# Accumulating three of the seven block products of a down projection in PSUM, in another order

## Chip, cores and metric

The kernel runs on one core of one Trainium2 chip. The metric is the device time of one execution in microseconds (us), the median of several runs.

## The reference

One layer of a causal decoder trunk on 1072 positions (16 meta tokens, 1024 prompt tokens, 8 x 4 new tokens), model width 1024, hidden width 2816:

```python
def swiglu(x, wg, wu, wd):
    return (jax.nn.silu(x @ wg) * (x @ wu)) @ wd
...
x = x + 0.5 * swiglu(rmsnorm(x, g1), w1g, w1u, w1d)
h = rmsnorm(x, gm)
...
x = x + jnp.concatenate([c, q], axis=-1) @ w_out + b_out
x = x + 0.5 * swiglu(rmsnorm(x, g2), w2g, w2u, w2d)
```

The change lies in the last product of the two SwiGLUs, the one with `wd`, the "down" product, and in its addition to x with the factor 0.5. All values are fp32.

## The kernel before

**Layout.** x is held transposed: channels on the 128 partitions (8 tiles of channels), positions along the free axis in three pieces of 358. `X(k, piece)` is one 128x358 tile of x. Each fp32 matrix operand is split into a high and a low part (`split`, L142 to L144: ScalarE casts the high part, VectorE or GpSimd subtracts it from the source for the low part), and a product is three matmuls per tile: high x high, high x low, low x high (`mul`, L129). For weights the low part is always made by GpSimd (`half_unit`, L167).

**Passes.** The first SwiGLU runs on the first two pieces of x in one pass, then on the third piece; the second one on its first piece and then on the other two in one pass. The passes on two pieces (`fast_pass`, L1095; "fast") save multiplications: a product of 2x2 blocks is made from seven block products m1 to m7 in place of eight, with sums of weight blocks and of data blocks as operands. `block_steps` (L522) takes the four weight blocks a11, a12, a21, a22 of such a product (two DMAs of 256 KB at a time), makes the sums on VectorE (`sums`, L534: L540 makes s1, L541 the operand of m7, L542 that of m6, L543 that of m3; m5 takes s1, m4 takes a22, m1 and m2 the raw a11 and a12) and hands each block product on.

**The down products.** In a fast pass, four pairs of hidden tiles after one another form a group with the following pair (`GROUPS`, L71), so there are four groups in each of the two passes. A group's hidden values are the data blocks b11, b21, b22, and the sums t1 to t4, made by `group_sink` (L679) as the up product of the group's second pair comes out. The names of the data operands in the profile are `xb` (b11 and b21), `hid0` and `hid1` (t2), `hid2` and `dt3l` (t3: high part in hid2, low part in dt3l), `dt1` (t1), `dt4` (t4), `db22` (b22). t3 is the last chain: VectorE subtracts b11's high part (L691) and its low part (L692) from b22's, ScalarE casts `hid2`, VectorE makes `dt3l` (L144). For each of two tiles i there is one such chain; that of i = 0 is made last and is the first one a product reads.

`fast_down` (L606) makes the down products of a group, once for each half j of the output channels: two blocks for each group, 16 in all. A block has seven products of two output tiles (`mp`) each, and each of these has six matmuls and takes one PSUM bank; there are eight banks (`pp`, L89). `OPERAND_OF` (L560) says which data operand a product takes. When a product is done, VectorE adds it to x at one or two places (L618), which the table `ADDS` (L603) lists. (A "twist" of x on GpSimd before and after the groups, L622, makes these additions enough.)

**Order.** `put_blocks` (L1079) puts the products in the order m1 with m2, m6, m7, m5, m4, m3 (`USUAL`, L1077). In `fast_pass` the gate product of the pair after the group stands ahead of the group's down products, and that pair's up product behind them. The planner loop (L1291) makes the weight operands of a step two steps ahead of its matmuls; there are six buffers for split weights (`W_BUFS`) and eight for raw blocks (`R_BUFS`). TensorE runs its matmuls in the order written (`keep_in_program_order`); the framework puts the instructions of the other engines in an order of its own by when it takes them to be ready, and each engine then works strictly in that order.

The gate product of the next pair leaves its results in PSUM: VectorE adds them up (L570) and ScalarE takes the Silu from the bank (L696, or L668 for a pair outside a group), which frees it.

Of the kernel before, what the change touches and what calls it, by code (L numbers as in the profile page):

```python
# [12 lines left out]
ALU = mybir.AluOpType  # L13
# [4 lines left out]
KH = KD // 2  # L18
# [66 lines left out]
def trunk(ctx: ExitStack, tc: tile.TileContext, xt, wf1, win, wout, wf2, wpool, vec, eye, sconv, spool,  # L85
          yt, ncp, npp, ncs, nps):
    nc = tc.nc
# [20 lines left out]
    def X(k, piece):  # L108

        a, b = piece  # L110
        return x[a // N][:, k, a % N : a % N + b - a]
# [8 lines left out]
    def accum():  # L120
        return pp.tile([P, 512], F32, name="acc", tag="acc")

    state = {"hid": -1, "raw": 0, "made": 0, "clock": 0.0}

    def matmul(acc, lhs, rhs, start, stop):
        tc.keep_in_program_order(nc.tensor.matmul(acc, lhs, rhs, start=start, stop=stop))  # L126
        state["clock"] += acc.shape[-1] / 2400.0

    def mul(accs, parts, start=True, stop=True):  # L129


        last = len(parts) - 1
        for i, (wh, wl, rh, rl) in enumerate(parts):
            for j, (lhs, rhs) in enumerate(((wh, rh), (wh, rl), (wl, rh))):
                at = 0
                for c, acc in enumerate(accs):
                    n = acc.shape[-1]
                    moving = rhs[c] if isinstance(rhs, list) else rhs[:, at : at + n]
                    matmul(acc, lhs, moving, start and i == 0 and j == 0, stop and i == last and j == 2)
                    at += n  # L140

    def split(hi, lo, src, engine=None):  # L142
# [376 lines left out]
            ups.append([plain(wsrc[4 * (f // 2) + f % 2], gate), plain(wsrc[4 * (f // 2) + 2 + f % 2], up)])  # L519
        return ups, [down_steps(wsrc, p, [piece], hid) for p in range(PAIRS)]  # L520

    def block_steps(src0, src1, product):  # L522

        st = {}

        def make0():
            st["r0"] = take(), take()
            return tuple(half_unit(r) for r in st["r0"])

        def use0(w):  # L530
            product("m1", w[0])
            product("m2", w[1])

        def sums():  # L534

            if "m4" in st:
                return
            (a11, a12), a21, a22 = st.pop("r0"), take(), take()
            s1 = pools["fast"].tile([P, KH, P], F32, name="sx", tag="sx", bufs=2)
            nc.vector.tensor_tensor(s1, a21, a22, ALU.add)  # L540
            nc.vector.tensor_tensor(a21, a11, a21, ALU.subtract)  # L541
            nc.vector.tensor_tensor(a11, s1, a11, ALU.subtract)  # L542
            nc.vector.tensor_tensor(a12, a12, a11, ALU.subtract)  # L543
            st.update(m5=s1, m6=a11, m7=a21, m3=a12, m4=a22)

        def made(name):
            def make():
                sums()
                return half_unit(st[name])
            return make  # L550

        def use_of(name):
            return lambda w: product(name, w)

        out = {"m12": ("step", [[(0, src0)]], make0, use0, False), "raw": [(0, src1)]}
        for name in ("m6", "m7", "m5", "m4", "m3"):
            out[name] = ("step", [], made(name), use_of(name), True)
        return out
# [3 lines left out]
    def fast_pair(src0, src1, get, n, sink):  # L562
# [23 lines left out]
        def product(name, w):  # L586
# [13 lines left out]

    ADDS = {"m1": ((0, 0, 1), (1, 1, 1)), "m2": ((0, 0, 1),), "m6": ((1, 1, 1),), "m7": ((1, 1, 1), (0, 1, 1)),  # L603
            "m5": ((1, 1, 1), (1, 0, 1)), "m4": ((1, 0, -1),), "m3": ((0, 1, -1),)}

    def fast_down(wsrc, p, j, pieces, ops):  # L606

        unit0 = 2 * F_TILES + 2 * p + 2 * j
        n = pieces[0][1] - pieces[0][0]

        def product(name, w):
            rh, rl = ops[OPERAND_OF[name]]
            for mp in range(2):
                acc = accum()[:, :n]
                mul([acc], [(w[0][:, 2 * mp + k], w[1][:, 2 * mp + k], rh[k], rl[k]) for k in range(2)])
                for r, c, sign in ADDS[name]:
                    to = X(j * KH + 2 * mp + r, pieces[c])
                    nc.vector.scalar_tensor_tensor(to, acc, 0.5 * sign, to, ALU.mult, ALU.add)  # L618

        return block_steps(wsrc[unit0], wsrc[unit0 + 1], product)  # L620

    def twist(pieces):  # L622

# [6 lines left out]
    def fast_ffn(wsrc, pieces, free, get, hid):  # L630
# [3 lines left out]
        n = N  # L634
# [44 lines left out]
        def group_sink(ops, second):  # L679
            silus, hs = {}, {}  # L680
            sub = nc.vector.tensor_tensor

            def put(name, i, t):
                if not ops:
                    ops.update(borrowed())
                if name not in ops:
                    ops[name] = own(name, 0), own(name, 1)
                split(ops[name][0][i], ops[name][1][i], t)

            def less(t, s, name, i):  # L690
                sub(t, s, ops[name][0][i], ALU.subtract)  # L691
                sub(t, t, ops[name][1][i], ALU.subtract)  # L692

            def gate(i, c, t):
                silus[i, c] = kept()
                nc.scalar.activation(silus[i, c], t, AF.Silu)  # L696

            def up(i, c, t):
                h = hs[i, c] = t if c else silus[i, c]
                nc.vector.tensor_tensor(h, t, silus[i, c], ALU.mult)  # L700
                if second:
                    put("b22" if c else "b21", i, h)
                elif c == 0:
                    put("b11", i, h)
                if (i, 1 - c) not in hs:
                    return
                if not second:
                    sub(hs[i, 1], hs[i, 1], hs[i, 0], ALU.subtract)
                    put("t1", i, hs[i, 1])
                    return  # L710
                b21, b22, t3 = hs[i, 0], hs[i, 1], temp()[:, :n]
                less(b22, b22, "t1", i)
                put("t2", i, b22)
                less(t3, b22, "b11", i)
                put("t3", i, t3)
                sub(b21, b21, b22, ALU.subtract)
                put("t4", i, b21)

            return gate, up

        for p in range(PAIRS):
            start = p if p in GROUPS else p - 1
# [288 lines left out]
    def got(key, what="h"):  # L1011
        def get():
            while what not in box[key] or (what != "pool" and not tasks[key].done):
                run_background(1, False)
            return box[key][what]
        return get
# [57 lines left out]
    fb1, fb1_d = plain_ffn(wf1, FFN1_B, got("h1b"))  # L1074
    fa2, fa2_d = plain_ffn(wf2, FFN2_A, got("h2a"))
    fb2, fb2_d, _ = fast_ffn(wf2, FFN2_B, 0, got("s2", "ops"), hid_b2)
    USUAL = ("m12", "m6", "m7", "m5", "m4", "m3")  # L1077

    def put_blocks(blocks, names=USUAL):  # L1079
        for name in names:  # L1080
            step = blocks[name]
            if blocks["raw"] is not None and name != "m12":
                step = (step[0], [blocks["raw"]]) + step[2:]
                blocks["raw"] = None
            plan.append(step)

    def put_down(d):

        for half in d:
            if isinstance(half, dict):  # L1090
                put_blocks(half)
            else:
                plan.append(half)

# [105 lines left out]
    last, room = {}, {}  # L1200
# [88 lines left out]
    i = 0  # L1289
# [103 lines left out]
```

## Time and profile before

| | |
|---|---|
| median of 3 runs | 1804.93 us (1803.71 to 1805.0) |
| profiled execution, its own time | 1803.07 us |
| its span, first to last instruction | 1801.3 us |
| mean granted TensorE clock | 0.986 |
| busy: TensorE, VectorE, ScalarE, GpSimd | 96%, 77%, 42%, 64% of the span |
| additions of down products to x (L618) | 320, busy 145.0 us |

The busy shares are means over the whole span. TensorE's share counts a stretch as busy while any matmul is in flight. A matmul of 358 columns shows some 328 ns in flight, and the next one starts about 164 ns after it, so the starts of matmuls tell more than their durations. An engine's idle time is shown with what ended it.

### The profile page before, as it was taken

The page shows a single profiled execution, that of the slowest core. Times are in us where ns is not written, and L with a number is a line of the kernel's source. Part 1 is how long each engine was busy: PE and PEld are TensorE (multiplying, and loading weights), DVE is VectorE, ACT ScalarE, POOL GpSimd, SP SyncE. Part 2 cuts the span into 40 slices and gives each one's busy share as a digit, 9 for nine tenths or more (in the row PEclk, how much of TensorE's full clock was granted, in tenths as well). Part 3 has the DMA queues.
Part 4 walks back from the last instruction along what each step waited for, and adds up shares of the span by engine and source line. Part 5 has one row for each costly group of instructions (what it writes and reads, how often), then busy time and mean ns, then how long its engine had stood idle before and what let it go on. Part 6 is the DMA issues. An engine that isn't in the chain of part 4 may idle for free.

```text
span 1801.3 us, 29876 instructions
## 1 busy us (share of the span) xinstructions
PE 1729.7 (96%) x10486; PEld 1712.5 (95%) x10486; DVE 1378.4 (77%) x2621; ACT 760.3 (42%) x1482; POOL 1146.0 (64%) x894
## 2 busy tenths in 40 slices
PE   6799999999999999999999998999999999999997
PEld 6799999999999999999999998999999999999997
DVE  8869898989747795897235888538587989898965
ACT  6444444443435224434234433545353434444444
POOL 5576766667745337667346657666577676767683
PEclk9899999999999999999999999999999999999998
DMA  6122232223353223443234494444332222222232
GB/s 209 35 83 71 71 103 82 72 77 98 103 118 119 65 67 115 124 135 111 66 106 129 126 135 133 126 134 123 111 105 91 71 83 71 82 71 72 70 100 83
DMA packets 115893, 177.70 MB, mean 99 GB/s; under 512 B 28320, under 2 KB 35744, under 8 KB 115744
## 3 DMA queue, kind: packets, MB, share of 16 engines
q1 hardware_dynamic: 115744, 175.80, 33.4%
q8 instruction: 83, 1.36, 0.3%
q14 instruction: 66, 0.54, 0.1%
HBM read 170.60 MB, written 5.15 MB: 98 GB/s over the span
## 4 chain that ended last, share of the span: by engine, by line
PE 75%; DVE 17%; issue 4%; DMA 2%; POOL 1%; ACT 1%; SPq 0%; DVEq 0%; POOLq 0%; ACTq 0%
PE acc L126 75%; DMA wraw<-in_wf 2%; DVE acc L265 2%; POOL wl L144 1%; DVE acc L814 1%; DVE wraw L542 1%; DVE acc L570 1%; DVE wraw L541 1%; DVE tmp L570 1%; DVE tmp L692 1%; DVE x L489 1%; DVE tmp L265 1%; DVE pr L832 1%; DVE wraw L543 0%; DVE xb L144 0%
## 5 line engine op out<-in xcount | busy, mean ns | idle before, releaser
L144 POOL TENSOR_TENSOR wl<-wraw,wh 128x512 fp32r<-128x512 f32 x740 | 991.3, 1350 | 588.9 <-ACT wh L143 541.7
L143 ACT CAST wh<-wraw 128x512 fp32r<-128x512 f32 x740 | 453.6, 621 | 685.6 <-PE acc L126 455.5
L126 PE MATMUL acc<-smt,wh 128*128 128x358 f32 x1024 | 253.1, 328 | 5.0 <-DVE mixl L144 4.0
L126 PEld LDWEIGHTS acc<-smt,wh 128*128 128x128 f32 x1024 | 181.7, 190 | 6.3 <-DVE mixl L144 4.6
L814 DVE SCALAR_TENSOR_TENSOR acc<-ub,vecs,acc 128x340 f32<-128x340 f32 (+2 forms) x348 | 183.5, 571 | 2.6
L126 PE MATMUL acc<-mixlt,wh 128*128 128x340 f32 x704 | 165.6, 319 | 2.6 <-DVE smt L144 2.4
L126 PE MATMUL acc<-smt,wl 128*128 128x358 f32 x512 | 167.8, 328 | 0.0
L489 DVE SCALAR_TENSOR_TENSOR x<-acc,x 128x358 f32<-128x358 f32 (+1 forms) x240 | 119.4, 517 | 35.0 <-PE acc L126 34.2
L618 DVE SCALAR_TENSOR_TENSOR x<-acc,x 128x358 f32<-128x358 f32 x320 | 145.0, 516 | 0.5 <-PE acc L126 0.4
L570 DVE TENSOR_TENSOR acc<-tmp,acc 128x358 f32<-128x358 f32 x168 | 85.7, 527 | 51.5 <-PE acc L126 48.2
L126 PEld LDWEIGHTS acc<-mixlt,wh 128*128 128x128 f32 x704 | 120.9, 188 | 3.4 <-DVE smt L144 2.7
L126 PE MATMUL acc<-mixlt,wl 128*128 128x340 f32 x352 | 112.1, 319 | 0.8 <-POOL wl L144 0.8
L144 POOL TENSOR_TENSOR wl<-sx,wh 128x512 fp32r<-128x512 f32 x58 | 85.5, 1475 | 30.5 <-ACT wh L143 28.7
L126 PEld LDWEIGHTS acc<-smt,wl 128*128 128x128 f32 x512 | 96.9, 189 | 0.0
L542 DVE TENSOR_TENSOR wraw<-sx,wraw 128x512 f32<-128x512 f32 x58 | 78.1, 1347 | 11.8 <-POOL wl L144 11.6
L126 PE MATMUL acc<-mixh,wh 128*128 128x356 f32 (+1 forms) x320 | 79.3, 328 | 4.7 <-DVE mixl L144 2.7
L126 PE MATMUL acc<-mixl,wh 128*128 128x356 f32 (+1 forms) x320 | 78.6, 327 | 0.0
L126 PE MATMUL acc<-mixh,wl 128*128 128x356 f32 (+1 forms) x320 | 78.5, 327 | 0.0
L541 DVE TENSOR_TENSOR wraw<-wraw 128x512 f32<-128x512 f32 x58 | 77.0, 1327 | 0.4
L570 DVE TENSOR_TENSOR tmp<-tmp,acc 128x358 f32<-128x358 f32 x126 | 65.4, 519 | 14.3 <-PE acc L126 13.1
L126 PE MATMUL acc<-b11h,wh 128*128 128x358 f32 x184 | 61.7, 335 | 10.8 <-ACT wh L143 10.8
L543 DVE TENSOR_TENSOR wraw<-wraw 128x512 f32<-128x512 f32 x58 | 70.4, 1214 | 2.0 <-POOL wl L144 1.5
(286 smaller groups left out, 4762.1 us busy)
## 6 DMA issues: line engine op xcount, KB each, us to landing
wraw<-in_wf SPq DMA_DIRECT2D x544, 256.0 KB, 2.9
wraw<-in_win SPq DMA_DIRECT2D x48, 256.0 KB, 2.7
wraw<-in_wout SPq DMA_DIRECT2D x32, 256.0 KB, 2.9
x<-in_xt SPq DMA_DIRECT2D x8, 179.0 KB, 4.3
tmp<-in_xt SPq DMA_DIRECT2D x8, 179.0 KB, 2.8
x<-in_xt SPq DMA_DIRECT2D x1, 1432.0 KB, 7.0
x<-in_xt SPq DMA_DIRECT2D x8, 178.0 KB, 5.0
out_yt<-tmp SPq DMA_DIRECT2D x8, 170.0 KB, 3.3
```

The costliest lines, as they stand in the source:

```text
L126: tc.keep_in_program_order(nc.tensor.matmul(acc, lhs, rhs, start=start, stop=stop))
L143: nc.scalar.copy(hi, src)
L144: (engine or nc.vector).tensor_tensor(lo, src, hi, ALU.subtract)
L265: nc.vector.scalar_tensor_tensor(t, X(k, piece), col(gain, k), r, ALU.mult, ALU.mult)
L489: nc.vector.scalar_tensor_tensor(X(m, piece), acc, 0.5, X(m, piece), ALU.mult, ALU.add)
L541: nc.vector.tensor_tensor(a21, a11, a21, ALU.subtract)
L542: nc.vector.tensor_tensor(a11, s1, a11, ALU.subtract)
L543: nc.vector.tensor_tensor(a12, a12, a11, ALU.subtract)
L570: nc.vector.tensor_tensor(t, s, acc, ALU.add)
L618: nc.vector.scalar_tensor_tensor(to, acc, 0.5 * sign, to, ALU.mult, ALU.add)
L692: sub(t, t, ops[name][1][i], ALU.subtract)
L814: nc.vector.scalar_tensor_tensor(to, src, w, part, ALU.mult, ALU.add)
```

## The change

In the down products (not in the gate and up products) m2 is accumulated in the PSUM bank that already holds m1, m3 in the bank of m7, and m4 in the bank of m5. VectorE adds m1, m7 and m5 to one place of x while they stand alone, and once more, to another place, when the second product has been accumulated on them. The order becomes m1, m7, m5, m2, m6, m3, m4. Two subtractions have their operands exchanged, so that m3 and m4 are added and not subtracted. m1 and m2 become steps of their own, though their weights are still split together.

```diff
-    def matmul(acc, lhs, rhs, start, stop):
-        tc.keep_in_program_order(nc.tensor.matmul(acc, lhs, rhs, start=start, stop=stop))
+    def matmul(acc, lhs, rhs, start, stop, more=False):
+        tc.keep_in_program_order(nc.tensor.matmul(acc, lhs, rhs, start=start, stop=stop, skip_group_check=more))
...
-    def block_steps(src0, src1, product):
+    def block_steps(src0, src1, product, turned=False):
...
-            nc.vector.tensor_tensor(a12, a12, a11, ALU.subtract)
+            nc.vector.tensor_tensor(a12, *((a11, a12) if turned else (a12, a11)), ALU.subtract)
...
-        out = {"m12": ("step", [[(0, src0)]], make0, use0, False), "raw": [(0, src1)]}
+        def make1():
+            st["w"] = make0()
+            return st["w"][0]
+
+        out = {"m12": ("step", [[(0, src0)]], make0, use0, False), "raw": [(0, src1)],
+               "m1": ("step", [[(0, src0)]], make1, use_of("m1"), False),
+               "m2": ("step", [], lambda: st["w"][1], use_of("m2"), False)}
...
-    ADDS = {"m1": ((0, 0, 1), (1, 1, 1)), "m2": ((0, 0, 1),), "m6": ((1, 1, 1),), "m7": ((1, 1, 1), (0, 1, 1)),
-            "m5": ((1, 1, 1), (1, 0, 1)), "m4": ((1, 0, -1),), "m3": ((0, 1, -1),)}
+
+    ADDS = {"m1": (1, 1), "m2": (0, 0), "m6": (1, 1), "m7": (1, 1), "m5": (1, 1), "m4": (1, 0), "m3": (0, 1)}
+    ON = {"m2": "m1", "m3": "m7", "m4": "m5"}
...
+        banks = {}
 
         def product(name, w):
             rh, rl = ops[OPERAND_OF[name]]
+            on = ON.get(name)
             for mp in range(2):
-                acc = accum()[:, :n]
-                mul([acc], [(w[0][:, 2 * mp + k], w[1][:, 2 * mp + k], rh[k], rl[k]) for k in range(2)])
-                for r, c, sign in ADDS[name]:
-                    to = X(j * KH + 2 * mp + r, pieces[c])
-                    nc.vector.scalar_tensor_tensor(to, acc, 0.5 * sign, to, ALU.mult, ALU.add)
-
-        return block_steps(wsrc[unit0], wsrc[unit0 + 1], product)
+                acc = banks[name, mp] = banks[on, mp] if on else accum()[:, :n]
+                mul([acc], [(w[0][:, 2 * mp + k], w[1][:, 2 * mp + k], rh[k], rl[k]) for k in range(2)],
+                    on is None, True, more=on is not None)
+                r, c = ADDS[name]
+                to = X(j * KH + 2 * mp + r, pieces[c])
+                nc.vector.scalar_tensor_tensor(to, acc, 0.5, to, ALU.mult, ALU.add)
+
+        return block_steps(wsrc[unit0], wsrc[unit0 + 1], product, True)
...
-                sub(b21, b21, b22, ALU.subtract)
+                sub(b21, b22, b21, ALU.subtract)
...
+    DOWN = ("m1", "m7", "m5", "m2", "m6", "m3", "m4")
     USUAL = ("m12", "m6", "m7", "m5", "m4", "m3")
...
-            if blocks["raw"] is not None and name != "m12":
+            if blocks["raw"] is not None and name not in ("m12", "m1"):
...
-                put_blocks(half)
+                put_blocks(half, DOWN)
```

## Rows read from the trace of the kernel before

**Rows 1.** The page's first part: busy time of each engine and its share.
```profile
PE 1729.7 (96%) x10486; PEld 1712.5 (95%) x10486; DVE 1378.4 (77%) x2621; ACT 760.3 (42%) x1482; POOL 1146.0 (64%) x894
```
**Rows 2.** Windows over the eight first blocks (j = 0): start:end, length, busy (count), clock.
```profile
240.26:256.94 16.68, 14.83 (x86) 13.68 (x85) 15.87 (x29) 9.01 (x19) 12.14 (x10) 1.00 0.32 96
...
1510.75:1526.30 15.55, 14.32 (x86) 13.74 (x85) 14.95 (x25) 6.51 (x13) 10.91 (x8) 1.00 0.22 69
...
1680.90:1698.35 17.45, 15.95 (x86) 15.26 (x85) 17.24 (x29) 6.99 (x14) 12.43 (x9) 0.90 0.20 62
sum 126.71, PE 116.54 PEld 111.46 DVE 123.46 ACT 54.46 POOL 89.11; mean PE 14.57 PEld 13.93 DVE 15.43 ACT 6.81 POOL 11.14
```
**Rows 3.** The same over the eight second blocks (j = 1).
```profile
1698.35:1712.14 13.79, 13.79 (x86) 13.79 (x85) 13.24 (x26) 4.15 (x7) 11.34 (x11) 1.00 0.24 76
sum 113.92, PE 112.67 PEld 110.80 DVE 112.64 ACT 34.32 POOL 93.06; mean PE 14.08 PEld 13.85 DVE 14.08 ACT 4.29 POOL 11.63
```
**Rows 4.** Timeline of TensorE in one group: start, length, operation, count, idle before.
```profile
1510.77 0.50 PE L126 MATMUL acc<-xb,wh 128*128 128x358 f32 x2
...
1517.35 0.43 PE L126 MATMUL acc<-hid0h,wh 128*128 128x358 f32 x1 [1.23 <-ACT cc L696]
...
1518.44 0.33 PE L126 MATMUL acc<-hid2h,wh 128*128 128x358 f32 x1
1518.60 0.32 PE L126 MATMUL acc<-dt3l,wh 128*128 128x358 f32 x1
...
1528.65 0.56 PE L126 MATMUL acc<-xb,wh 128*128 128x358 f32 x2 [0.20 <-DVE x L618]
```
**Rows 5.** Timeline of VectorE in that group.
```profile
1487.39 0.54 DVE L570 TENSOR_TENSOR acc<-tmp,acc 128x358 f32<-128x358 f32 x1 [3.48 <-PE acc L126]
...
1510.60 0.68 DVE L541 TENSOR_TENSOR wraw<-wraw 128x512 f32<-128x512 f32 x1
1511.20 1.62 DVE L692 TENSOR_TENSOR tmp<-tmp,xb 128x358 f32<-128x358 f32 x1
...
1513.18 1.19 DVE L144 TENSOR_TENSOR dt4l<-cc,dt4h 128x358 fp32r<-128x358 f32 x1
...
1514.73 1.18 DVE L144 TENSOR_TENSOR dt3l<-tmp,hid2h 128x358 fp32r<-128x358 f32 x1
...
1517.58 3.58 DVE L618 SCALAR_TENSOR_TENSOR x<-acc,x 128x358 f32<-128x358 f32 x8
```
**Rows 6.** Timeline of VectorE, t3's low part in the second group of pass one.
```profile
240.81 0.53 DVE L144 TENSOR_TENSOR dt3l<-tmp,hid2h 128x358 fp32r<-128x358 f32 x1
```
**Rows 7.** Instructions of single lines: count, shortest/median/longest in ns, first and last start.
```profile
L618 DVE SCALAR_TENSOR_TENSOR x<-acc,x x320: 512/515/532, 162.2 to 1714.8; 128x358 f32<-128x358 f32 x160
...
L692 DVE TENSOR_TENSOR tmp<-tmp,xb x16: 519/1312/1623, 148.0 to 1681.7; 128x358 f32<-128x358 f32 x16
...
L144 DVE TENSOR_TENSOR dt3l<-tmp,hid2h x8: 534/1176/1181, 159.4 to 1685.2; 128x358 fp32r<-128x358 f32 x8
```
**Rows 8.** Timeline of GpSimd beside those VectorE instructions.
```profile
1510.76 1.67 POOL L144 TENSOR_TENSOR wl<-wraw,wh 128x512 fp32r<-128x512 f32 x1 [0.95 <-PE acc L126]
```
**Rows 9.** Windows of 12 us that begin with a long wait of TensorE.
```profile
553.20:565.20 12.00, 9.80 (x60) 9.50 (x59) 8.49 (x17) 8.10 (x20) 7.38 (x6) 1.00 0.27 91
584.60:596.60 12.00, 9.33 (x47) 8.80 (x46) 6.94 (x14) 3.63 (x9) 4.12 (x3) 0.86 0.15 49
821.80:833.80 12.00, 10.24 (x54) 9.83 (x52) 9.58 (x19) 4.37 (x9) 9.27 (x9) 0.86 0.38 110
856.80:868.80 12.00, 9.94 (x62) 9.44 (x61) 4.95 (x10) 4.96 (x10) 3.57 (x3) 1.00 0.16 55
994.00:1006.00 12.00, 9.60 (x60) 9.33 (x59) 7.58 (x15) 6.53 (x14) 7.54 (x6) 1.00 0.32 96
1241.60:1253.60 12.00, 9.33 (x51) 9.05 (x50) 12.00 (x26) 6.79 (x15) 7.01 (x7) 0.86 0.35 109
```

More of the change, by code (lines that the diff above doesn't have):

```diff
@@ L123, in trunk, with mul @@
     state = {"hid": -1, "raw": 0, "made": 0, "clock": 0.0}
-    def matmul(acc, lhs, rhs, start, stop):
-        tc.keep_in_program_order(nc.tensor.matmul(acc, lhs, rhs, start=start, stop=stop))
+    def matmul(acc, lhs, rhs, start, stop, more=False):
+        tc.keep_in_program_order(nc.tensor.matmul(acc, lhs, rhs, start=start, stop=stop, skip_group_check=more))
         state["clock"] += acc.shape[-1] / 2400.0
-    def mul(accs, parts, start=True, stop=True):
+    def mul(accs, parts, start=True, stop=True, more=False):
         last = len(parts) - 1
@@ L138, in mul @@
                     moving = rhs[c] if isinstance(rhs, list) else rhs[:, at : at + n]
-                    matmul(acc, lhs, moving, start and i == 0 and j == 0, stop and i == last and j == 2)
+                    matmul(acc, lhs, moving, start and i == 0 and j == 0, stop and i == last and j == 2,
+                           more)
                     at += n
```

## The prediction

> **What bounds the kernel now.** The page's first part comes first: TensorE is busy 96% of the span, VectorE 77% [rows 1]. Work taken off VectorE is worth only what TensorE now waits for it, so the next view is the length of each stretch that the change touches. Each of the 16 down blocks has 84 matmuls. The one block without a wait lasts 13.79 us, 0.164 us for a matmul [rows 3]. The eight first blocks of the groups (j = 0) last 126.71 us together [rows 2], 16.4 more than 8 x 13.79; the eight second ones 113.92 [rows 3], 3.6 more. So 20.0 us of waits stand in all down blocks, 1.1% of the span, and that is the most that relief of VectorE can give.
>
> The timelines of one group tell what these waits are. The first block begins at 1510.77. At 1517.35 TensorE has idled 1.23 us for the Silu of the gate product before it [rows 4]: the sixth PSUM bank that the block asks for still holds a gate result. VectorE is behind by then, with work of the up and gate products; it begins the first addition to x at 1517.58 [rows 5]. So none of this group's additions stands ahead of that wait, and those of the group before don't either, since VectorE idled 3.48 us until 1487.39 [rows 5]. Only the wait in the second block, at 1528.65, is one for additions to x (0.20 us of idle, released by L618) [rows 4].
>
> **Additions.** Ten additions become seven, times two output tiles and 16 blocks: 320 less 224 leaves 96 fewer. Eight of them in a row take 3.58 us [rows 5], each lasts 0.515 [rows 7], so one follows another after (3.58 - 0.52) / 7 = 0.44 us, and VectorE is relieved of 42 us. What comes of that on TensorE's path is the wait of the second blocks: 3.6 us before, of which I leave 0.5 for small matmuls of the next pass's norm that run inside one of them (an estimate). Term: **-3.1 us**. The rest of the 42 us is idle time of an engine that TensorE doesn't wait for. The first blocks' waits don't move by it.
>
> **Order.** m7 moves from fourth to second place, and its data operand is t3. In the group shown m7 reads t3 at 1518.44 and 1518.60 (high and low part) [rows 4], long after VectorE has made the low part, which it begins at 1514.73 and ends 1.18 later, at 1515.91 [rows 5]. In second place m7's first matmul would be due 12 x 0.164 after 1510.77, at 1512.74, and the second, which reads that low part, at 1512.90. It can't start before 1515.97 (0.06 for the signal, an estimate). All of TensorE's queue stands behind that matmul: m7, m5, m2, m6, m3, m4 and the up product. The delay is 3.07 us; with two slow restarts of about 0.1 each, 3.3. The bank at 1517.35 is no second wait then, since the sixth bank would be asked for at 1510.77 + 30 x 0.164 + 3.3 = 1519.0. So 3.3 us takes the place of the 1.76 us (15.55 - 13.79) that a regular first block loses now [rows 2].
>
> Of the eight low parts of t3, seven look like this one: the median lasts 1176 ns [rows 7], and the last begins at 1685.2 [rows 7], 4.3 us after its block's start at 1680.90 [rows 2]. In the second group of pass one it begins at 240.81 and lasts 0.53 [rows 6], 0.55 after the block's start [rows 2]; there is no new wait, and the block keeps the 2.9 us of bank waits that it has (16.68 - 13.79) [rows 2]. New first blocks: 7 x 3.3 + 2.9 = 26.0 against 16.4. Term: **+9.6 us**.
>
> **The clock.** A long wait of TensorE is in some cases followed by a stretch at the lower of its two levels (1.2 in place of 2.4 GHz). Of the six windows that begin with a wait of about 2 to 3 us, three have a mean granted clock of 0.86 and three of 1.00 [rows 9]. One of the eight first blocks has such a stretch now: 17.45 us long, granted 0.90 [rows 2], which is 1.7 us of clock lost at most; I take 1.5. Seven new waits at one chance in two: **+5.2 us**, with 0 and 10.5 as ends. (The 3.3 of the last group holds no such stretch, so its present one is already taken out.)
>
> **Banks.** m2 now waits for VectorE's addition of m1 out of the same bank; m6, m3, m4 stand behind it on TensorE, and on VectorE the additions of m2 and the next block's weight sums. Before, a bank came round after four products (8 us); m2 now follows m1 after three. The first addition ends 0.52 after 1517.58, 7.3 us into the block [rows 5]. m2 is due at 36 x 0.164 + 3.3 = 9.2, so it finds its bank read. Cost 0; without t3's wait m2 would be due at 5.9 + 1.8 = 7.7, still 0.4 later. The Trainium skill, PSUM — Partial Sum Buffer, in its summary for kernel authors, says "Evacuate promptly", and it speaks against this part: six of eight banks are now held for three products and more. By that rule m2 would wait and the sum would be that of the third rival; the rows have banks as the limit only at the sixth request, and the new order asks for no new bank at m2.
>
> **The rest.** Two subtractions change sides: 0. Steps m1 and m2 share a weight split as before, and the four raw blocks of a product are fetched in the same order, so no DMA and no wait of SP's queue is added; m6's raw block is freed two conversions later and m7's one earlier, with eight buffers to hide it. m2's split weights are held 4 us longer in one of six buffers; the cover is that a buffer comes free every product (2 us) and that GpSimd's conversion takes 1.67 at most here [rows 8]; without it, such a time per block, 27 us in all.
>
> **The uncertain size** is when t3 comes. VectorE's instructions with two operands in SBUF last 0.52 or up to 1.62 us (L692) [rows 7], and the long ones lie beside GpSimd's conversions [rows 5, 8]. Were none slowed, L692, dt4l and dt3l would save 1.10 + 0.67 + 0.66 = 2.4 us and t3 would come at 1513.5; were L541 and two other weight sums ahead of it, 0.68 now [rows 5], slowed as L692 is, some 2.8 later. ScalarE's cast for m7 no longer waits for L542's sum, so conversions may move either way. I take no shift: the two ends are equally far.
>
> **Sum.** -3.1 + 9.6 + 5.2 = +11.7 us. The profiled execution took 1803.07 us (span 1801.3 and 1.8 around it), 1.9 below the median, which gives 1814.8; I say **1815**. (From the median it would be 1816.6.)
>
> **Rivals.**
> - *t3 in time.* If its low part comes more than 0.9 us earlier, then 7 x 2.4 + 2.9 + 0.5 = 20.2 is no more than the waits of now, and the change pays. For it: the conversions beside it are laid out anew. Against: it has the same place among VectorE's work, and none of that ahead of it is removed. With t3 1.0 to 2.4 us earlier and no lower clock, 1794 to 1802; at 1.6 earlier, 7 x 1.7 + 3.4 = 15.3, or 1798.4.
> - *VectorE's relief clears all waits.* 20 us less, 1783; a good half of it, 1790. Against it: VectorE is behind before the group's first addition.
> - *Held banks.* m1's additions are put behind the next block's sums on VectorE (two of up to 1.7 us), so m2 waits 1 to 3 us in each first block, on top of t3: 8 x 1 to 3 on 1815, 1823 to 1839. Decided by whether the addition of m1 ends before 9.2 us into the block.
> - *Balance.* t3 0.5 to 1 us earlier and the clock never lower: 1801 to 1806. That the change doesn't do what it says isn't likely: matmuls keep their written order, and the additions are counted.
>
> **Chances.** Forecast, t3 late, 0.52 (own range 1807 to 1826); held banks 0.08; balance 0.13; t3 in time 0.21, a third of it within 0.2%; all waits cleared 0.06. A measurement of this kernel can tell about 0.2%, 3.6 us, from no change. Faster 0.20, same 0.20, slower 0.60. The range, 1799 to 1826, leaves out the cleared waits (0.06), the earliest t3 (about 0.07) and the top of the held banks (0.05).
>
> **What would show it.** Right: first matmuls of m7 with `dt3l` idle some 2.5 us for VectorE at 7 of 8 groups; first blocks of about 17.1 us (18.6 with a lower clock), second ones of 13.8; 224 additions. Wrong: m7 starts without idle time, or the first blocks keep the wait for the Silu, or m2 is released by L618.

## The result and the profile after

The changed kernel takes 1830.53 us, the median of 4 runs (1827.02 to 1831.47), against 1804.32 for the kernel before (4 runs, 1803.42 to 1805.0): a ratio of 1.014, 95% interval 1.0125 to 1.0156. It is slower, as predicted, but by 26 us and not by 10, and outside the range. The profiled execution took 1831.12 us; its span is 1829.3, 28.0 more than before. The change shifts the lines of the file: the additions to x are L630 (L618 before), the four weight sums L542 to L545 (L540 to L543), the casts L144 and the low parts L145 (L143 and L144).

Two lines of the page answer to [rows 1] and [rows 7]. The page's first part, and its group of the additions (busy time, mean ns of one, idle time of VectorE ahead of them and what ended it):

```profile
PE 1741.7 (95%) x10486; PEld 1725.7 (94%) x10486; DVE 1367.2 (75%) x2525; ACT 761.6 (42%) x1482; POOL 1146.1 (63%) x894
...
L630 DVE SCALAR_TENSOR_TENSOR x<-acc,x 128x358 f32<-128x358 f32 x224 | 108.2, 519 | 29.2 <-PE acc L126 29.1
```

The 96 additions are gone, and VectorE now stands idle for 29.1 us ahead of the ones that are left, waiting for TensorE. That is what relief of an engine looks like when nobody waited for it.

The windows over the eight first blocks (j = 0), to be read beside [rows 2]: start:end, length, busy time and count of each engine, granted clock.

```profile
157.53:176.10 18.57, 15.87 (x86) 15.33 (x85) 16.94 (x27) 6.83 (x14) 12.92 (x9) 0.91 0.19 57
245.09:261.83 16.74, 14.88 (x86) 13.70 (x85) 14.97 (x25) 9.28 (x19) 13.48 (x10) 1.00 0.33 104
333.17:353.76 20.59, 16.89 (x86) 16.35 (x85) 18.03 (x29) 7.89 (x15) 12.96 (x9) 0.83 0.17 56
...
1529.79:1549.32 19.53, 15.87 (x86) 15.33 (x85) 17.96 (x28) 7.88 (x15) 12.93 (x9) 0.91 0.18 57
...
sum 154.29, PE 127.68 PEld 122.70 DVE 139.68 ACT 63.36 POOL 101.52; mean PE 15.96 PEld 15.34 DVE 17.46 ACT 7.92 POOL 12.69
```

And over the second blocks (j = 1), beside [rows 3]:

```profile
1549.32:1563.11 13.79, 13.79 (x86) 13.79 (x85) 11.54 (x20) 4.35 (x7) 9.58 (x8) 1.00 0.19 61
...
sum 112.02, PE 111.49 PEld 110.91 DVE 92.99 ACT 34.51 POOL 84.06; mean PE 13.94 PEld 13.86 DVE 11.62 ACT 4.31 POOL 10.51
```

First blocks: 154.29 - 126.71 = +27.6 us. Second blocks: 112.02 - 113.92 = -1.9. That is 25.7 of the 28.0 us; about 1.2 more lies ahead of the first group and 1.2 between the groups of the first pass and those of the last. Seven first blocks are long, and all seven have a mean granted clock under 1; the one of the second group is as long as before and at 1.00.

The timeline of TensorE in the group that [rows 4] shows, now beginning at 1529.81 (in brackets the idle time and what ended it):

```profile
1529.81 0.50 PE L126 MATMUL acc<-xb,wh 128*128 128x358 f32 x2
...
1531.62 0.33 PE L126 MATMUL acc<-xb,wl 128*128 128x358 f32 x1
1533.52 0.43 PE L126 MATMUL acc<-hid2h,wh 128*128 128x358 f32 x1 [1.57 <-ACT hid2h L144]
1536.03 0.43 PE L126 MATMUL acc<-dt3l,wh 128*128 128x358 f32 x1 [2.08 <-DVE dt3l L145]
...
1536.49 0.50 PE L126 MATMUL acc<-hid2l,wh 128*128 128x358 f32 x1
1536.79 0.50 PE L126 MATMUL acc<-dt3l,wh 128*128 128x358 f32 x1
```

m7's first matmul waits for t3's high part, its second one for the low part. It starts 6.22 us into the block; twelve matmuls of m1 and one of m7, at 0.164 each, would have had it start at 2.13. The delay is 4.1 us. VectorE's timeline tells why it isn't the 3.07 that was worked out, to be read beside [rows 5]:

```profile
1524.98 1.78 DVE L544 TENSOR_TENSOR wraw<-sx,wraw 128x512 f32<-128x512 f32 x1
1526.69 1.77 DVE L542 TENSOR_TENSOR sx<-wraw 128x512 f32<-128x512 f32 x1
...
1531.34 1.60 DVE L704 TENSOR_TENSOR tmp<-tmp,xb 128x358 f32<-128x358 f32 x1
...
1533.30 1.16 DVE L145 TENSOR_TENSOR dt4l<-cc,dt4h 128x358 fp32r<-128x358 f32 x1
...
1534.83 1.15 DVE L145 TENSOR_TENSOR dt3l<-tmp,hid2h 128x358 fp32r<-128x358 f32 x1
...
1537.65 1.39 DVE L630 SCALAR_TENSOR_TENSOR x<-acc,x 128x358 f32<-128x358 f32 x3
```

t3's low part ends at 1535.98, 6.17 us into the block, where it was 5.14 before [rows 5]. L704, dt4l and dt3l are as long as they were (1.62, 1.19 and 1.18 in [rows 5]). What is new stands ahead of them: the sum L542 (s1 of the next block's weights) takes 1.77 us. In the kernel before, the timelines of the same place have 0.68 for it, with GpSimd at rest beside it and ScalarE waiting:

```profile
1505.95 1.77 DVE L542 TENSOR_TENSOR wraw<-sx,wraw 128x512 f32<-128x512 f32 x1
1507.65 0.68 DVE L540 TENSOR_TENSOR sx<-wraw 128x512 f32<-128x512 f32 x1
```
```profile
1505.83 1.35 POOL L144 TENSOR_TENSOR wl<-wraw,wh 128x512 fp32r<-128x512 f32 x1 [1.51 <-ACT wh L143]
1508.51 1.30 POOL L144 TENSOR_TENSOR wl<-wraw,wh 128x512 fp32r<-128x512 f32 x1 [1.33 <-ACT wh L143]
```

```profile
1507.81 0.62 ACT L143 CAST wh<-wraw 128x512 fp32r<-128x512 f32 x1 [1.35 <-DVE wraw L542]
```

GpSimd's pause from 1507.18 to 1508.51 is a wait for ScalarE's cast, and the cast waits for the sum ahead of L540, L542 (L544 now), which makes the weights of m6. With m7 in second place the weights converted there were summed a block earlier, and GpSimd runs on in the changed kernel, 1524.87 to 1527.91, beside both sums:

```profile
1524.87 3.04 POOL L145 TENSOR_TENSOR wl<-wraw,wh 128x512 fp32r<-128x512 f32 x2 [1.52 <-ACT wh L144]
```

The second of these two conversions ends at 1527.91, and the s1 sum, begun beside it, ends 0.55 us behind that, at 1528.46. ScalarE is not what slows the sum: in the kernel before, its cast at 1507.81 runs beside the short one. Counted over the whole trace of the changed kernel, 76 of the 232 weight sums begin while GpSimd rests, and they last 0.68 to 0.69 us; the other 156 begin while a GpSimd instruction runs, and none of them ends sooner than 0.54 us after that instruction's end (median 0.55).

So the s1 sum loses 1.1 us, and everything behind it on VectorE, t3 among it, comes 1.0 us later.

### The profile page after: what moved, and what is told of

It reads as the page before. It is cut to its first block, busy times and chain, and to the rows that moved or that the text cites. A ratio compares the mean times of both kernels' runs of the same rounds, so it can differ in the third digit from the quotient of the medians.

```text
span 1829.3 us, 29726 instructions
## 1 busy us (share of the span) xinstructions
PE 1741.7 (95%) x10486; PEld 1725.7 (94%) x10486; DVE 1367.2 (75%) x2525; ACT 761.6 (42%) x1482; POOL 1146.1 (63%) x894
## 4 chain that ended last, share of the span: by engine, by line
PE 74%; DVE 20%; issue 3%; ACT 1%; DMA 1%; POOL 0%; SPq 0%; DVEq 0%; ACTq 0%; POOLq 0%
PE acc L126 74%; DVE wraw L544 2%; DVE acc L266 2%; DVE acc L578 1%; DVE tmp L704 1%; DVE wraw L543 1%; DVE acc L826 1%; DVE tmp L578 1%; DMA wraw<-in_wf 1%; DVE x L490 1%; DVE tmp L266 1%; DVE pr L844 1%; DVE dt3l L145 1%; DVE cc L712 0%; DVE xb L145 0%
## 5 line engine op out<-in xcount | busy, mean ns | idle before, releaser
L145 POOL TENSOR_TENSOR wl<-wraw,wh 128x512 fp32r<-128x512 f32 x740 | 995.7, 1356 | 588.8 <-ACT wh L144 545.5
L144 ACT CAST wh<-wraw 128x512 fp32r<-128x512 f32 x740 | 455.6, 621 | 682.0 <-PE acc L126 483.8
L630 DVE SCALAR_TENSOR_TENSOR x<-acc,x 128x358 f32<-128x358 f32 x224 | 108.2, 519 | 29.2 <-PE acc L126 29.1
L145 POOL TENSOR_TENSOR wl<-sx,wh 128x512 fp32r<-128x512 f32 x58 | 81.5, 1406 | 53.9 <-ACT wh L144 51.2
L544 DVE TENSOR_TENSOR wraw<-sx,wraw 128x512 f32<-128x512 f32 x58 | 73.8, 1272 | 16.5 <-POOL wl L145 16.3
L543 DVE TENSOR_TENSOR wraw<-wraw 128x512 f32<-128x512 f32 x58 | 79.1, 1364 | 0.4
L545 DVE TENSOR_TENSOR wraw<-wraw 128x512 f32<-128x512 f32 x58 | 78.3, 1351 | 0.1
L542 DVE TENSOR_TENSOR sx<-wraw 128x512 f32<-128x512 f32 x58 | 68.7, 1184 | 13.0 <-DMA wraw<-in_wf 12.4
```

What stands on the lines that cost most here:

```text
L144: nc.scalar.copy(hi, src)
L145: (engine or nc.vector).tensor_tensor(lo, src, hi, ALU.subtract)
L545: nc.vector.tensor_tensor(a12, *((a11, a12) if turned else (a12, a11)), ALU.subtract)
L630: nc.vector.scalar_tensor_tensor(to, acc, 0.5, to, ALU.mult, ALU.add)
```

## The experiments

Each was timed beside the kernel before on the same chip, whose median there was 1806 to 1808 us. "First" and "second" are the sums of the eight blocks each in the profiled execution; before they are 126.71 and 113.92.

**The order alone.** The order of the change with the ten additions of before, nothing accumulated.

```diff
-    ADDS = {"m1": (1, 1), "m2": (0, 0), "m6": (1, 1), "m7": (1, 1), "m5": (1, 1), "m4": (1, 0), "m3": (0, 1)}
-    ON = {"m2": "m1", "m3": "m7", "m4": "m5"}
+    ADDS = {"m1": ((1, 1), (0, 0)), "m2": ((0, 0),), "m6": ((1, 1),), "m7": ((1, 1), (0, 1)),
+            "m5": ((1, 1), (1, 0)), "m4": ((1, 0),), "m3": ((0, 1),)}
+    ON = {}
...
-                r, c = ADDS[name]
-                to = X(j * KH + 2 * mp + r, pieces[c])
-                nc.vector.scalar_tensor_tensor(to, acc, 0.5, to, ALU.mult, ALU.add)
+                for r, c in ADDS[name]:
+                    to = X(j * KH + 2 * mp + r, pieces[c])
+                    nc.vector.scalar_tensor_tensor(to, acc, 0.5, to, ALU.mult, ALU.add)
```

> The changed kernel's order m1, m7, m5, m2, m6, m3, m4, but each product in a bank of its own and ten additions as before. Theory (order alone): first blocks of 19.5 us and more with 1.9 and 2.5 us waits for hid2h and dt3l in seven groups, second blocks back at 14.1 to 14.3; 1828 to 1836 us. Rival (accumulation): within 0.3% of the kernel before, 1799 to 1810 us.

Measured: 1832.67 us, ratio 1.0145 (1.0131 to 1.0159), first 155.82, second 112.10. The order alone makes the whole loss. Against what I expected, it also makes the small gain: the second blocks come down to 13.79 us with all ten additions. The delay in the first block lets VectorE catch up; the additions that the change saves bring nothing that can be measured.

**t3 out of the way.** m7 reads the operand t1 in place of t3, so the output is not the reference's; the number of operations is the same.

```diff
-            rh, rl = ops[OPERAND_OF[name]]
+            rh, rl = ops["t1" if name == "m7" else OPERAND_OF[name]]
```

> The changed kernel, but m7 of the down products reads t1, which is ready long before, in place of t3, which no matmul then reads (t3 is still made). Same instructions, order and banks. Theory: the 1.9 and 2.5 us waits vanish, the wait for the sixth bank comes back at about 6.5 us into the block; first blocks 15.3 to 15.8, second ones 13.8; 1799 to 1804 us. Rival (m7's weights or banks are late, not t3): a wait at the same matmul stays, 1815 us or more.

Measured: 1817.38 us, ratio 1.006 (1.0046 to 1.0074), first 132.06, second 115.45. The theory has the waits right and the time too low. No wait for t3 is left and no first block has a clock under 1.00, so t3 with its clock costs 154.29 - 132.06 = 22.2 us in the first blocks. But a first block still takes 16.65 us, 1.1 more than the 15.55 of before. Its waits, from the timeline of TensorE in one group:

```profile
1525.07 0.43 PE L126 MATMUL acc<-dt1h,wh 128*128 128x358 f32 x1 [0.54 <-DVE tmp L578]
...
1526.61 0.43 PE L126 MATMUL acc<-dt1h,wh 128*128 128x358 f32 x1 [0.28 <-DVE tmp L578]
...
1529.08 0.43 PE L126 MATMUL acc<-dt1h,wh 128*128 128x358 f32 x1 [1.22 <-ACT cc L708]
```

These are the banks of the gate product. The sixth request is met 7.70 us after the block's start at 1521.38, where it was 6.58 before [rows 4], since VectorE is 1.1 us later with what frees them. So the slow s1 sum would cost the block a microsecond even if t3 were in time. The first blocks make 5.4 of the 12.7 us that this span (1814.0) is longer than before. In the second blocks, 1.5 us longer together, m7's bank waits for an addition (0.7 us from start to start in five of them), with seven additions in place of ten. The largest other part, 5.1 us, lies between the two passes and stays open (see the end of this section).

**m7 third.** One product more between the block's start and m7, accumulation kept.

```diff
-    DOWN = ("m1", "m7", "m5", "m2", "m6", "m3", "m4")
+    DOWN = ("m1", "m5", "m7", "m2", "m6", "m4", "m3")
```

> The order m1, m5, m7, m2, m6, m4, m3, accumulation kept: m7 is due one product (2.0 us) later than in the change. Theory (the loss is what t3 is late beyond m7's place): of the 4.2 us by which a late first block is delayed, some 2.0 to 2.2 go, so first blocks take 16.9 to 17.5 us in place of 19.5 to 20.6, second ones 13.8; 1811 to 1818 us, and no lower clock behind the wait in most groups. Rival (held banks set the time): m2 still stands on m1's bank with one product in between and m4, m3 on banks freed late by VectorE, so first blocks stay near the 18.4 of the run with m7 fourth, and the time at 1824 to 1830.

Measured: 1816.8 us, ratio 1.0055 (1.004 to 1.007), first 135.72, second 113.98. As the theory has it: two microseconds of room take most of t3's wait away (0.59 us of idle is left in the group at 1519.93), and m2 doesn't wait for its bank (two products stand between it and m1, not one as the expectation says). A first block without a lower clock takes 16.63, no more than with t3 out of the way: what is left of t3's wait replaces part of the waits for the gate product's banks. The clock does something that I hadn't looked for. Two windows over first blocks with the same pattern of waits:

```profile
1433.26:1450.96 17.70, 16.21 (x86) 15.11 (x85) 16.59 (x25) 7.79 (x15) 13.14 (x9) 0.90 0.21 63
1519.93:1536.56 16.63, 14.85 (x86) 13.75 (x85) 15.52 (x23) 7.69 (x15) 12.21 (x9) 1.00 0.20 64
```

Three of eight first blocks are at 0.90 or 0.91, five at 1.00; one of the five, in the second group, has no wait for t3.

**m7 fourth.** Room enough for t3, accumulation kept.

```diff
-    DOWN = ("m1", "m7", "m5", "m2", "m6", "m3", "m4")
+    DOWN = ("m1", "m5", "m6", "m7", "m2", "m4", "m3")
```

> The changed kernel with the order m1, m5, m6, m7, m2, m4, m3: still seven additions and three products accumulated on others, m7 in the fourth place that it had before. Theory (the loss is m7 asked for before t3 is there, and the clock that falls after that wait): no wait for dt3l; seven of the first blocks 15.5 to 15.7 us as before (the wait for the sixth bank stays), second blocks 13.8; 112.0 in place of 113.9 us there, so 1800 to 1803 us. Rival (held banks or the accumulation itself cost the time): 1815 us or more, with m2 or m4 waiting for L630.

Measured: 1825.12 us, ratio 1.010 (1.0087 to 1.0114), first 146.91, second 110.96. The rival's side, though not with the product that it names: no matmul waits for t3, but m3, accumulated on m7 with m2 and m4 between, waits for the additions of m7 in six of the eight first blocks (the other two have a mean clock of 0.91). A regular first block takes 18.45 us: 1.8 more than with t3 out of the way, whose waits for the gate product's banks it has too. The two waits in TensorE's timeline, and VectorE's:

```profile
1541.26 0.40 PE L126 MATMUL acc<-db22h,wh 128*128 128x358 f32 x1 [0.95 <-DVE x L630]
...
1542.86 0.43 PE L126 MATMUL acc<-db22h,wh 128*128 128x358 f32 x1 [0.35 <-DVE x L630]
```
```profile
1533.41 2.71 DVE L630 SCALAR_TENSOR_TENSOR x<-acc,x 128x358 f32<-128x358 f32 x6
1537.22 1.75 DVE L544 TENSOR_TENSOR wraw<-sx,wraw 128x512 f32<-128x512 f32 x1 [1.11 <-POOL wl L145]
1538.90 1.78 DVE L542 TENSOR_TENSOR sx<-wraw 128x512 f32<-128x512 f32 x1
1540.60 0.52 DVE L630 SCALAR_TENSOR_TENSOR x<-acc,x 128x358 f32<-128x358 f32 x1
1541.04 1.32 DVE L543 TENSOR_TENSOR wraw<-wraw 128x512 f32<-128x512 f32 x1
1542.29 0.52 DVE L630 SCALAR_TENSOR_TENSOR x<-acc,x 128x358 f32<-128x358 f32 x1
```

VectorE has a fixed order, and in it m7's two additions stand behind the next block's sums, the first of which waits 1.11 us for a conversion by GpSimd. VectorE ends the six additions at 1536.1 and comes to m7's first one at 1540.6.

**m6 second, two orders.** Here m6's conversion should make GpSimd pause again.

```diff
-    DOWN = ("m1", "m7", "m5", "m2", "m6", "m3", "m4")
+    DOWN = ("m1", "m6", "m7", "m2", "m5", "m3", "m4")
```

> The order m1, m6, m7, m2, m5, m3, m4, accumulation kept. Theory: with m6 in second place the conversion of its weights waits again for the third of the four weight sums, so the first sum goes back from 1.77 to about 0.7 us and t3 comes 1.1 us earlier; m7 is then due about 2.0 us later than in the change, so its wait falls from 4.2 to about 1.1 us and no clock is lost; first blocks 15.0 to 16.5 us, second ones 13.8; 1799 to 1809 us. Rival (held banks, additions standing behind the next block's sums on VectorE): m2 or m3 waits for its addition by 1 us and more in each first block, first blocks 17.5 to 19; 1814 to 1827 us.

```diff
-    DOWN = ("m1", "m7", "m5", "m2", "m6", "m3", "m4")
+    DOWN = ("m1", "m6", "m5", "m2", "m7", "m4", "m3")
```

> The order m1, m6, m5, m2, m7, m4, m3, accumulation kept: m7 is in fifth place, due at 7.9 us, and t3 can't be late. Theory of the shift (the first weight sum is slow because the second product's weights are converted beside it): that sum takes 0.6 to 0.8 us as in the kernel before, VectorE's chain runs 1.1 us earlier than with m7 fourth, and the waits for banks go back to about 1.4 us a block; first blocks 15.2 to 17.1 us, 1802 to 1812 us. If the slow sum has another cause, it stays at 1.77 us and first blocks stay near 18.4 us, 1822 to 1827. The rival of held banks expects waits of 0.5 to 1.5 us at m3 on m7's bank, which shows in the release by an addition to x.

Measured: 1855.17 us, ratio 1.027 (1.0253 to 1.0286), first 166.79, second 123.55; and 1856.03, ratio 1.0269 (1.0253 to 1.0285), first 166.54, second 124.23. Both forecasts of the time fell, by 44 us and more; the rivals name the held banks, but their times are too low as well. The part on the sum holds: in VectorE's timeline of the second of the two it is short again, with GpSimd's pause of 1.34 us beside it:

```profile
1541.22 1.78 DVE L544 TENSOR_TENSOR wraw<-sx,wraw 128x512 f32<-128x512 f32 x1
1542.92 0.68 DVE L542 TENSOR_TENSOR sx<-wraw 128x512 f32<-128x512 f32 x1
...
1550.01 1.18 DVE L145 TENSOR_TENSOR dt3l<-tmp,hid2h 128x358 fp32r<-128x358 f32 x1
```
```profile
1541.10 1.34 POOL L145 TENSOR_TENSOR wl<-wraw,wh 128x512 fp32r<-128x512 f32 x1 [1.51 <-ACT wh L144]
1543.78 1.29 POOL L145 TENSOR_TENSOR wl<-wraw,wh 128x512 fp32r<-128x512 f32 x1 [1.34 <-ACT wh L144]
```

And t3 comes earlier with it: its low part ends at 1551.19, 5.2 us after the block's start at 1546.01, as in the kernel before. That settles the cause of the shift. In every run here that has m6 or m2 behind m1, that sum takes 0.68 us in this group and t3 ends 5.1 to 5.2 us into the block; in every run that has m7 or m5 there, 1.77 to 1.78, and t3 ends at 6.2 to 6.3.

What ate the gain is the held bank, with a lower clock behind it (0.85 to 0.98 in the first blocks of both). m4 on m5 in the first order, m3 on m7 in the second, have one product between them, and each waits once in a first block for an addition. The second order's wait in TensorE's timeline:

```profile
1563.32 0.64 PE L126 MATMUL acc<-db22h,wh 128*128 128x358 f32 x1 [3.50 <-DVE x L630]
```

Most second blocks, which had no such wait in the runs so far, have one too (1.4 us from start to start in five of eight, 0.7 in two, in both orders).

**m2 at once.** To price the wait for a bank directly: m2 stands right behind m1.

```diff
-    DOWN = ("m1", "m7", "m5", "m2", "m6", "m3", "m4")
+    DOWN = ("m1", "m2", "m6", "m7", "m5", "m4", "m3")
```

> The changed kernel with the old order m1, m2, m6, m7, m5, m4, m3, m2 accumulated on m1 straight after it, m4 straight after m5. This prices the wait for a bank that is to be read before it is accumulated on. Theory (VectorE reaches its first addition some 7 us into a first block): m2 waits about 5.4 us there and m4 some 0.5 us; 20 us for a first block with the clock's part, about 14.8 for a second one; 1840 to 1860 us. Rival (the read of a bank in the middle costs little): under 1812 us.

Measured: 1897.02 us, ratio 1.0503 (1.0489 to 1.0518), first 188.33, second 143.08, far above what was written. m2's wait in a regular first block is near what was written (5.5 us from start to start, 5.4 written). m4's isn't: 0.5 us was written, and it is 1.5 to 2.0 there and 3.3 to 3.7 in six second blocks. The mean clock is below 1.00 in all first blocks and in five second ones. In TensorE's timeline m2 is ready at 1569.1, and the first addition of the block begins at 1573.90, 6.8 us into the block as in [rows 5]:

```profile
1574.47 0.97 PE L126 MATMUL acc<-xb,wh 128*128 128x358 f32 x2 [5.20 <-DVE x L630]
```

**The change in the second blocks alone.** The first blocks keep order and additions of before (`TEN` lists the ten).

```diff
...
-            on = ON.get(name)
+            on = ON.get(name) if j else None
...
-                r, c = ADDS[name]
...
+                for r, c in (ADDS[name],) if j else TEN[name]:
...
-                put_blocks(half, DOWN)
+                put_blocks(half, DOWN if j else USUAL)
```

> The change in the second blocks (j = 1) alone: the first blocks (j = 0) have the order and the ten additions of before. Theory: the whole loss lies in the first blocks and the gain of the additions in the second, so first blocks last 126 to 128 us together as before, second ones 110.5 to 112.5 (before 113.9); 1801 to 1804 us by the profiled execution's scale of 1803, that is 1 to 3.5 us under the kernel before. Rival (moving t3 and the conversions delays VectorE in every block): second blocks lose too, or the next group's first blocks do, and the time is 1806 to 1815 us.

Measured: 1812.51 us, ratio 1.003 (1.0018 to 1.0041), first 124.51, second 120.29. The rival's side. The first blocks are those of before, the one late stretch of lower clock left out [rows 2]; the second ones lose 0.8 us each where 0.3 were to be gained. Without a late first block VectorE is still at the additions of that block, and the banks of the second block's first products come late: the waits at 1536.39 and 1538.18 are released by additions (0.07 and 0.53 us of idle). The slow s1 sum is here too, now ahead of the first block's last additions. VectorE's timeline, then that of the kernel before in the same place, then TensorE's wait:

```profile
1531.96 1.78 DVE L542 TENSOR_TENSOR sx<-wraw 128x512 f32<-128x512 f32 x1
```
```profile
1523.52 0.69 DVE L540 TENSOR_TENSOR sx<-wraw 128x512 f32<-128x512 f32 x1 [0.36 <-DMA wraw<-in_wf]
```
```profile
1538.18 0.40 PE L126 MATMUL acc<-hid2h,wh 128*128 128x358 f32 x1 [0.53 <-DVE x L632]
```

In the change this is hidden by the delay ahead of it.

**One accumulation in the old order.** m3 on m7's banks, with m5 and m4 between; nine additions.

```diff
...
-    ON = {"m2": "m1", "m3": "m7", "m4": "m5"}
+    ON = {"m3": "m7"}
...
-                put_blocks(half, DOWN)
+                put_blocks(half)
```

> The order of before (m1 and m2 as one step, m6, m7, m5, m4, m3) with one accumulation alone: m3 on m7's banks, two products (m5, m4) in between, nine additions in place of ten. t3's wait and the change of order are out of it. Theory (a held bank costs, because VectorE puts m7's addition behind the next block's weight sums): m3 waits 0.8 to 2 us for an addition to x in each first block, first blocks 16.3 to 17.5 us, second ones 13.8 to 14.1; 1807 to 1821 us. Rival (the accumulation by itself is free, and the loss of the change is its order alone): first blocks stay at 15.5 to 15.6 us, 1801 to 1806 us, no matmul on db22h waits.

Measured: 1810.59 us, ratio 1.0021 (1.0011 to 1.0032), first 133.81, second 111.08. The theory's side. Order and t3 are as before, and the accumulation by itself costs the first block 1.1 us (16.65 against 15.55), by the same pattern as with m7 fourth. VectorE's timeline, then TensorE's:

```profile
1524.21 3.58 DVE L631 SCALAR_TENSOR_TENSOR x<-acc,x 128x358 f32<-128x358 f32 x8
1528.03 1.77 DVE L544 TENSOR_TENSOR wraw<-sx,wraw 128x512 f32<-128x512 f32 x1 [0.24 <-POOL wl L145]
1529.72 0.68 DVE L542 TENSOR_TENSOR sx<-wraw 128x512 f32<-128x512 f32 x1
1530.33 0.52 DVE L631 SCALAR_TENSOR_TENSOR x<-acc,x 128x358 f32<-128x358 f32 x1
1530.77 1.67 DVE L543 TENSOR_TENSOR wraw<-wraw 128x512 f32<-128x512 f32 x1
1532.36 0.52 DVE L631 SCALAR_TENSOR_TENSOR x<-acc,x 128x358 f32<-128x358 f32 x1
```
```profile
1532.93 0.44 PE L126 MATMUL acc<-db22h,wh 128*128 128x358 f32 x1 [0.71 <-DVE x L631]
```

The second addition of m7 stands behind the sum L543, and m3's second tile waits for it.

**The same in the second blocks alone.** What it adds to the edit of the run before this one (`TEN` lists the ten additions):

```diff
...
-            on = ON.get(name)
+            on = ON.get(name) if j else None
...
-                for r, c in ADDS[name]:
+                for r, c in (ADDS if j else TEN)[name]:
```

> As the run with m3 on m7's banks in the old order, but in the second blocks (j = 1) alone; the first blocks have their ten additions of before. Question: are the second blocks at 13.8 us because VectorE has fewer additions, or because the first blocks came to their end later and VectorE had caught up? If fewer additions do it: first blocks 124.5 to 126.7 us together, second ones 13.8 each (111 together), 1799 to 1804 us, under the kernel before by 1 to 4 us. If the delay did it: second blocks stay at 14.1 us or wait about 1 us more for m7's additions at m3 (14.1 to 15.1 each), 1803 to 1813 us.

Measured: 1805.41 us, ratio 0.9988 (0.9977 to 1.0), first 125.01, second 115.11. Seven of the eight second blocks stay at 14.1 to 15.2 us, as before, and one takes 15.29: the waits there are for additions of the first block (0.43 us from start to start at 1530.73), which this version doesn't touch, and in the longest one also for a converted weight. Nothing is won by it that can be told from no change, and no version tried beats the kernel before.

One thing stays open. Between the groups of the first pass and those of the last lies work that no experiment touches, and it takes 1.2 us more in the change, 0.2 with the order alone, 1.0 with m2 at once and 2 to 5.3 in the eight variants between 1805 and 1857 us. In six of these eight TensorE waits for a converted weight between 1074 and 1085 us, 2.0 to 3.5 us from start to start; but with the order alone it waits 2.5 us there too, so this isn't shown to be the cause. What moves it wasn't tried; it is as large as the smaller differences between blocks here, so what is said of mechanisms rests on the lengths of the blocks, and a small ratio of whole times doesn't price one.

## Why the prediction was wrong, point by point

The kernel is slower in the way that was written, m7 waiting for t3 and the clock falling behind that wait. What failed is the size of two terms: the step "The uncertain size", which put the shift of t3 at nothing, and the clock, put at one chance in two.

**What bounds the kernel: right.** The waits of the first blocks are not for additions, and 96 fewer of them don't move those waits; the order alone has the ratio of the whole change (1.0145 and 1.014, with intervals that overlap almost wholly).

**Additions: the size was near, the reason wasn't.** -1.9 us against -3.1. The second blocks reach 13.79 as written (one, of the second group, doesn't). But the order alone reaches it with ten additions, and the second blocks with nine additions behind first blocks of the old length don't, so it is the delay that gives it and not the relief. That the term came out near is luck.

**Order: right in kind, under-sized.** t3 is late in seven groups and in time in the second, m7's second matmul waits for `dt3l`, and in the seven the wait for the Silu is gone. The waits of the seven blocks come to 27.8 us (start to start, less 0.164 each) where 7 x 3.3 = 23.1 was written: +4.7. The step that failed is **"The uncertain size"**: "I take no shift: the two ends are equally far." The measured shift is +1.0 us. The sentence ahead of it, that the cast for m7 no longer waits for the sum, had the cause in hand; followed one step on, it says that GpSimd then runs beside the next sum, and that sums begun beside GpSimd are the long ones. Nor are the seven alike, as was written: the wait is 4.1 us in six groups and 3.1 in the first. There t3's low part, which begins at 159.4 in the kernel before [rows 7], 3.0 us into the block, comes 1.0 us earlier in the block than in the group of the timelines, in both kernels. The Trainium skill, SBUF — State Buffer, "Who interferes with whom", has VectorE's second pair of ports shared with GpSimd under an exclusive lock; the trace agrees, with 0.68 us for the sum while GpSimd rests, and 1.77 beside it, to 0.55 us behind the end of the conversion.

**The clock: under-sized.** "One chance in two" came from single waits in other passes [rows 9]. All seven late blocks had the lower level (1.2 GHz) for a while (in the group of the timelines matmuls start 0.30 us apart from 1536.49 on, in place of 0.164), the third and fourth group for longer. Windows of 12 us from the wait on, for the third group and for that of the timelines:

```profile
333.00:345.00 12.00, 8.30 (x35) 7.76 (x34) 10.06 (x18) 5.41 (x11) 7.27 (x5) 0.72 0.18 59
...
1531.60:1543.60 12.00, 8.34 (x41) 7.80 (x40) 10.43 (x17) 4.38 (x10) 7.91 (x6) 0.86 0.20 66
```

The seven blocks exceed 7 x 13.79 by 41.0 us, of which 27.8 are the waits; 13.2 are left for the clock, 1.9 a block, where 5.2 was written: +8.0, the larger of the two misses. Both factors were low: seven of seven in place of one in two, and 1.9 us in place of 1.5.

**The sum.** 11.7 + 4.7 + 8.0 + 1.2 (additions) + 2.4 (outside the blocks) gives the 28.0 of the spans. The prediction doesn't say how its upper end, 1826, is made up. In its own terms the clock in all seven blocks alone would give 1820 and a shift of 1 us in them alone 1822, both inside the range; the two together give 1815 + 7 + 5.3 = 1827, outside it.

**Banks: right for this order.** No product waits for an addition in the change's first blocks, and none does there with t3 out of the way. But the cover is thinner than "cost 0" sounds: where the bank's reader stands behind the next block's sums, two products in between left a wait that costs 1.1 us a block (one accumulation in the old order), and one in between left 3.8.

**The rivals.** "t3 in time" would not have paid with the slow sum in place: with t3 out of the way a first block still loses 1.1 us, because that sum delays the gate product's banks too. (The whole kernel is then 0.6% slower; 5.1 of the 12.7 us of its longer span lie in work whose delay stays open.) "Held banks" is not what happened, though the measured 1830.5 lies in the time that it gives, 1823 to 1839; but it is what each attempt to give t3 more room ran into, apart from m7 third.

## What to carry to other kernels

When a product is moved, follow its weights as well as its data: the conversion that no longer waits may run beside an instruction of another engine and slow it (here a weight sum, from 0.68 to 1.77 us), and with a fixed order everything behind that one comes late. Accumulating on a result that is also read alone makes the reader's place in its engine's queue part of TensorE's path; look for what stands ahead of that read before counting the reads saved. Two unknown terms that push the same way belong into one end of the range together.

## What the runs showed that I had not expected

The granted clock doesn't follow from one wait alone. In the change it fell in 7 of 7 blocks in which a wait of 2.5 us (start to start) comes one matmul behind another, of 1.9 us in six of them and 0.9 in the first group. With m7 third, where the wait for t3 is about 1.0 us, it left four of the seven first blocks with that wait at 1.00 and three at 0.90 or 0.91. With t3 out of the way none fell, with waits of 0.9, 0.6 and 1.55 us for banks; with m7 fourth, which has the same three waits, two first blocks are at 0.91. What tells the ones from the others wasn't found.

The price of a held bank isn't a matter of the number of products between the pair. With two in between, m2 on m1 waits for nothing in the change and with m7 third, and m3 on m7 waits with m7 fourth and in the old order; with one in between it is 3.8 us from start to start in two different orders. What decides is what VectorE has queued ahead of the read.
